# Two blocks on one core: taps moved to TensorE, scaled rows before transposes, head squares in parts

## The chip, the cores and the metric

The kernel runs on one core of one Trainium2 chip. The metric is the device time of one execution in microseconds (us), smaller is better. All tensors that go in and come out are float32.

## The reference, cut to what matters

1,024 tokens of 1,024 channels go through two blocks, one after the other.

```python
def first_block(x):            # names shortened
    h = rmsnorm(x, g); p = h @ w_in                      # 3,072 columns
    d = diff_attention(4 heads, 128 wide); d = rmsnorm(d per head)
    r = silu(gate) * head_rmsnorm(retention(4 heads, 128 wide))
    x = x + concat(d, r) @ w_out
    return x + hier_moe(rmsnorm(x))                      # 32 experts, top 2
def second_block(x):
    h = rmsnorm(rmsnorm(x) of the block before, a_g)     # two norms in a row
    u, v = split(h @ a_w_in + b); g = u * sigmoid(v)     # 8 tiles of 128 channels
    g = depthwise causal convolution of 31 taps over the tokens, per channel
    s = silu(layer_norm(g)); x = x + s @ a_w_out + b
    return x + relu(rmsnorm(x) @ w1) ** 2 @ w2           # 4,096 wide
```

## The kernel before, in words

Nearly every matrix product is a sum of three matmuls on fp32r operands: each float32 operand is split into a rounded upper part (a copy on ACT) and a rest (a subtraction on DVE, for some weights on POOL); `split` and `mm3` (lines 34 to 43) do it. A few products stay plain float32 matmuls on PE.

Phase 1 is the first block up to the router: projections and heads (1a), then `w_out` and the router (1b). Each of the eight heads ends in a norm over its 128 channels, which lie on the partitions. `head_norms` (line 285) squares a head's 128x512 tile on ACT (`osq`), and PE sums the squares over the partitions with a float32 matmul against a matrix of 1/128 (`pm`, line 291, 16 of them in all). Phase 2 runs the 32 experts. Phase 3 (line 1300 on) is the second block.

Phase 3 works on two blocks of 512 tokens, b = 0 and b = 1, and on eight channel tiles, ct = 0 to 7. Its stages, in the order of the driver at the end of the function:

- `first_norms(n)` for n = 0 to 3, 256 tokens each: loads rows `h` (a DMA on POOL), sums squares on ACT (the `junk` activations), makes the reciprocal root on DVE (a chain of twelve small operations, `rs`), and then turns rows into columns on PE (`pt`), from which ACT and DVE write the two parts `xh` and `xl`. Before, the scale of a row enters as a diagonal matrix `dg`: a float32 matmul of the rows against `dg` scales and turns at once. The rows are also scaled in place (`s`) and stored (`x2d`) for the residual.
- `a_in(ct, b)`: two products of 24 matmuls each (`pin`), a sigmoid on ACT (`sig`) and the gated product on DVE (`g`).
- the 31 taps of each channel tile (`conv_steps`). On DVE a tap is one multiply-add over 128x512 (`pc` or `cv`). For ct 4 of b = 0 ACT and POOL do it. For the tiles in `PE_TAPS` a number of the taps of b = 0 run on PE: ACT builds a diagonal of the tap's coefficients, and PE adds a float32 matmul of it with the shifted columns into PSUM.
- `ln(b)`: turns the tiles into rows (`pl`), takes mean and variance on DVE, scales (`cvT`), turns back, silu.
- `a_out(b)`: the product `po`, the residual in `acc`, sums of squares, the reciprocal root, and rows turned to columns with a diagonal per 128 tokens (`pt` again).
- `mlp(b, q)`: products `pf` and `py`; at the last q the results go out by DMA.

Each engine works in order through its own queue. Which instruction stands where in the queues of phase 3 is set by the order in which the code issues and by the scheduler's estimates; two counters of work on PE and DVE (`Counted`) decide how many taps are issued between two products, and `hold()` ties the following instructions of an engine behind the last one. `fill` is a generator that hands out the four products that are kept back from `a_in` of b = 1 for ct 6 and 7; three of its pieces are issued inside `ln(0)` and the last one during `a_out(0)`. Weights (`raw`, three buffers) are split into `whl` on ACT, and then on DVE or, for weights 4 to 15 (`POOL_W`), on POOL.

## Time and profile before

| | us |
|---|---|
| median of 3 runs | 2219.58 |
| lowest, highest | 2219.05, 2225.35 |
| profiled execution, device time | 2219.59 |
| its span | 2217.9 |
| PE busy in the span | 2139.9 (96%) |
| DVE busy | 1631.0 (74%) |
| ACT busy | 1166.6 (53%) |
| POOL busy | 222.2 (10%) |

The span starts with the first instruction and ends with the last; 1.7 us of the device time lie around it. The first 600 us are phases 1a and 1b (they meet at 433 us), the experts end at 1155 us, and phase 3 takes the rest. A matmul on float32 operands leaves two records in the trace, one on fp32r operands one.

### The profile page before, as it was taken

Reading aid. Unit: us, or ns where it says so; the run is one execution under the profiler, and the core shown is the slowest. Engines: PE = TensorE matmul, PEld = TensorE weight load, DVE = VectorE, ACT = ScalarE, POOL = GpSimd, SP = SyncE. Lnnn points to the kernel's source line nnn. Section 1 sums busy time; section 2 is a strip of 40 time slices with the busy share of each in tenths; the row PEclk is TensorE's granted clock in tenths of the full one; section 3 lists DMA queues with packets and bytes.
Section 4 is the critical chain, followed back from the end, with each engine's and each line's share of the span. In section 5 each row is a group of like instructions: output and inputs, shape, how many; then the busy total and the mean of one; then the engine's idle time right before and its main releaser. Section 6 shows DMA issues by size and latency. Waiting matters only on the chain.

```text
span 2217.9 us, 28289 instructions
## 1 busy us (share of the span) xinstructions
PE 2139.9 (96%) x10561; PEld 1743.1 (79%) x10562; DVE 1631.0 (74%) x2538; ACT 1166.6 (53%) x1633; POOL 222.2 (10%) x214
## 2 busy tenths in 40 slices
PE   6999999999699999999988998999999999999998
PEld 5888888788577777777757886988888898888887
DVE  7788755665799999999978998899996634443442
ACT  5565544522588888888866352344333434333431
POOL 0000000010211111121111370000000000000000
PEclk9999999999799999999999999999999999999999
DMA  4111112277799999999974311233332434233331
GB/s 156 41 39 45 49 49 64 80 260 271 284 371 369 359 366 365 358 357 351 367 248 143 101 39 48 77 93 107 105 95 76 126 97 149 86 97 94 108 98 42
DMA packets 194128, 367.62 MB, mean 166 GB/s; under 512 B 15104, under 2 KB 137408, under 8 KB 169408
## 3 DMA queue, kind: packets, MB, share of 16 engines
q1 hardware_dynamic: 177040, 318.01, 41.4%
q0 software_dynamic: 16944, 47.74, 6.7%
q8 instruction: 85, 1.39, 0.3%
q14 instruction: 59, 0.48, 0.1%
HBM read 342.62 MB, written 35.65 MB: 171 GB/s over the span
## 4 chain that ended last, share of the span: by engine, by line
PE 45%; issue 21%; DVE 3%; DMA 3%; ACT 1%; POOL 0%; POOLq 0%; ACTq 0%; DVEq 0%; SPq 0%
PE pin L1265 7%; PE py L1265 6%; PE pf L1265 5%; PE pg L38 5%; PE pg L37 5%; PE pg L36 5%; PE py L36 2%; PE py L38 2%; PE py L37 2%; DMA h<-y,src 2%; PE po L1265 1%; PE pt L1093 1%; DVE cv L1265 1%; PE pt L1265 1%; PE pl L1265 1%
## 5 line engine op out<-in xcount | busy, mean ns | idle before, releaser
L1062 DVE TENSOR_TENSOR wl<-raw,wh 128x1024 fp32r<-128x1024 f32 x384 | 454.4, 1220 | 39.4 <-PE pg L37 24.6
L1061 ACT ACTIVATE wh<-raw 128x1024 fp32r<-128x1024 f32 x384 | 395.9, 1058 | 49.8 <-PE pg L38 27.8
L1265 PE MATMUL py<-whl,hid 128*128 128x512 f32 x1536 | 360.4, 392 | 0.3 <-ACT hid L1265 0.2
L1265 ACT ACTIVATE whl<-raw 128x1024 fp32r<-128x1024 f32 x160 | 168.5, 1057 | 339.4 <-PE py L1265 125.0
L1265 PEld LDWEIGHTS py<-whl,hid 128*128 128x128 f32 x1536 | 285.0, 188 | 65.8 <-ACT hid L1265 5.2
L1265 PE MATMUL pf<-xh,whl 128*128 128x512 f32 x1024 | 318.8, 390 | 0.3 <-DVE whl L1265 0.3
L1265 DVE TENSOR_TENSOR whl<-raw,whl 128x1024 fp32r<-128x1024 f32 x148 | 180.4, 1228 | 144.5 <-ACT whl L1265 143.9
L1265 PEld LDWEIGHTS pf<-xh,whl 128*128 128x128 f32 x1024 | 192.1, 188 | 40.2 <-DVE whl L1265 0.5
L36 PE MATMUL pg<-wh,xth 128*112 128x512 f32 x512 | 204.7, 400 | 0.0
L38 PE MATMUL pg<-wh,xtl 128*112 128x512 f32 x512 | 201.9, 394 | 0.0
L37 PE MATMUL pg<-wl,xth 128*112 128x512 f32 x512 | 201.2, 393 | 0.4 <-DVE wl L1062 0.4
L1265 PE MATMUL pf<-xl,whl 128*128 128x512 f32 x512 | 199.5, 390 | 0.0
L1265 PE MATMUL pin<-xh,whl 128*128 128x512 f32 (+1 forms) x544 | 164.9, 383 | 6.7 <-ACT xh L1265 6.6
L1265 DVE SCALAR_TENSOR_TENSOR cv<-g,cols,cv 128x512 f32<-128x512 f32 x232 | 161.5, 749 | 0.0
L36 PE MATMUL pp<-xhl,wh 128*128 128x512 f32 x384 | 156.6, 408 | 0.0
L37 PE MATMUL pp<-xhl,wh 128*128 128x512 f32 x384 | 151.6, 395 | 0.0
L38 PE MATMUL pp<-xhl,wl 128*128 128x512 f32 x384 | 150.6, 392 | 0.0
L1265 DVE TENSOR_TENSOR acc<-acc,py 128x512 f32<-128x512 f32 x128 | 87.5, 685 | 84.5 <-PE py L1265 84.0
L1265 DVE SCALAR_TENSOR_TENSOR pc<-g,cols,pc 128x512 f32<-128x512 f32 x194 | 135.6, 752 | 3.2 <-ACT pc L1265 1.6
L1265 PEld LDWEIGHTS pin<-xh,whl 128*128 128x128 f32 x544 | 100.8, 190 | 26.1 <-ACT xh L1265 7.8
L1265 ACT ACTIVATE relu<-pf 128x512 f32<-128x512 f32 x64 | 38.0, 594 | 140.0 <-PE pf L1265 137.3
L1265 PEld LDWEIGHTS pf<-xl,whl 128*128 128x128 f32 x512 | 96.2, 188 | 19.8
(435 smaller groups left out, 3859.8 us busy)
## 6 DMA issues: line engine op xcount, KB each, us to landing
raw<-in_expert_w_gate_dram SPq DMA_DIRECT2D x64, 1024.0 KB
raw<-in_expert_w_up_dram SPq DMA_DIRECT2D x64, 1024.0 KB
raw<-in_expert_w_down_dram SPq DMA_DIRECT2D x64, 1024.0 KB
raw<-in_mlp_w_dram SPq DMA_DIRECT2D x128, 512.0 KB
wst<-in_w_in_dram SPq DMA_DIRECT2D x24, 512.0 KB
raw<-in_a_w_in_dram SPq DMA_DIRECT2D x16, 512.0 KB
raw<-in_a_w_out_dram SPq DMA_DIRECT2D x16, 512.0 KB
x<-in_x_dram SPq DMA_DIRECT2D x8, 512.0 KB
```

The costliest lines, as they stand in the source:

```text
L36: nc.tensor.matmul(out, lhsT=ah, rhs=bh, start=first, stop=False)
L37: nc.tensor.matmul(out, lhsT=ah, rhs=bl, start=False, stop=False)
L38: nc.tensor.matmul(out, lhsT=al, rhs=bh, start=False, stop=last)
L1061: s.acts.append(nc.scalar.activation(th, src, AF.Copy))
L1062: lo = nc.vector.tensor_tensor(tl, src, f32(th), op=ALU.subtract)
L1093: last = nc.tensor.transpose(pt[:, j], c.xg[e % XG][:CAP, (4 * q + j) * 128:(4 * q + j + 1) * 128], c.ident[:CAP, :CAP])
L1265: return s.placed(f(*args, **kw))
```

## The change

1. `head_norms`: the matrix of 1/128 is fp32r. Each tile of squares is split into two fp32r parts (`osp`: a copy on ACT, a subtraction on DVE), and two fp32r matmuls take the place of one float32 matmul, 16 times.
2. `PE_TAPS` goes from 10 taps of ct 7 to 8 taps of ct 6 and 20 taps of ct 7, so 28 taps of b = 0 run on PE.
3. `first_norms` and `a_out` no longer build diagonals. Rows are scaled into another tile first, on ACT or DVE (`scaled`), and PE turns them with its transpose operation: 64 transposes in `first_norms`, 64 in the two `a_out`.
4. The driver takes the statistics and the scaling of n = 2 ahead of the second half of `a_in(0, 0)`, and those of n = 3 right behind it.
5. `fill`: two pieces ahead of the layer norm's transposes, one held between their first and second half, and the last one now at the end of `a_out(0)`.
6. The eight last outputs of b = 1 go out from SP's queue and no longer from POOL's.

```diff
-        c.ones_mean = cst2.tile([128, 128], F32, name="ones_mean")
-        V.memset(c.ones_mean, 1.0 / 128)
+        ones = sm.tile([128, 128], F32, tag="state", bufs=2, name="ones")
+        V.memset(ones, 1.0 / 128)
+        c.ones_mean = cst2.tile([128, 128], F32R, name="ones_mean")
+        V.tensor_copy(c.ones_mean, ones)
...
-                nc.tensor.matmul(pm[:, z], lhsT=c.ones_mean, rhs=sq, start=True, stop=True)
+                sp_ = sp.tile([128, 2, 512], F32R, tag="cs0", bufs=4, name="osp")
+                split(nc, sp_[:, 0], sp_[:, 1], sq)
+                for y in range(2):
+                    nc.tensor.matmul(pm[:, z], lhsT=c.ones_mean, rhs=sp_[:, y], start=y == 0, stop=y == 1)
...
-PE_TAPS = {7: 10}
+PE_TAPS = {6: 8, 7: 20}
...
+        def scaled(y, x, r, z):
+            if z:
+                A.activation(y, x, AF.Copy, scale=r)
+            else:
+                V.tensor_scalar(y, x, r, None, op0=ALU.mult)
+            return y
...
-            for j, (y, dg) in enumerate(zip(ys, dgs)):
-                nc.tensor.matmul(pt[:, j * 128:j * 128 + 128], lhsT=y[:, k * 128:(k + 1) * 128], rhs=dg, start=True, stop=True)
+            for j, y in enumerate(ys):
+                nc.tensor.transpose(pt[:, j * 128:j * 128 + 128], y, c.ident)
...
-            dgs = [diagonal(rs[:, 0, 1, z:z + 1]) for z in range(2)]
+            ys = [scaled(h[:, z], s[:, z], rs[:, 0, 1, z:z + 1], z or n) for z in range(2)]
...
-            dgs = [diagonal(rs[:, 0, j:j + 1]) for j in range(4)]
+            ys = []
+            for z in range(2):
+                ys.append([gp[b].tile([128, GW], F32, tag="g", name="y")[:, :512] for _ in mine])
+                for j, i in enumerate(mine):
+                    scaled(ys[z][j], acc[i][:, z * 512:z * 512 + 512], rs[:, 0, j:j + 1], j % 2)
...
-                        nc.gpsimd.dma_start(out=out[0, i * 128:i * 128 + 128, d], in_=acc[i][:, d])
+                        (nc.sync if b else nc.gpsimd).dma_start(out=out[0, i * 128:i * 128 + 128, d], in_=acc[i][:, d])
...
+        next(norm[2])
+        next(norm[2])
         run(a_in(0, 0, 256, 512))
+        next(norm[3])
+        next(norm[3])
         nc.level()
-        next(norm[2])
         run(a_in(1, 0), LEAD, (0,))
         next(norm[2])
-        next(norm[3])
-        next(norm[2])
         run(a_in(2, 0), LEAD, (0,))
-        next(norm[3])
         next(norm[3])
...
         next(fill)
+        next(fill)
         pump(1e9, (0,))
         V.hold()
         for n, _ in enumerate(steps):
-            if n == 0:
-                for _ in range(3):
-                    next(fill)
+            if n == 3:
+                nc.tensor.hold()
+                next(fill)
```

How the queues of phase 3 move is shown at two places. The first is ACT's queue near the start, around the split of the weights for the second product of `a_in(2, 0)`: `whl_13085` in the kernel before. `pin_12946` is the first product of `a_in(1, 0)`, and `pt_13045` to `pt_13072` are the turned rows of n = 2. Before:

```order
L1265 ACTIVATE pc_12971<-g_12769,cols_1181 128x512
L1265 ACTIVATE whl_13085<-raw_12937 128x1024
L1265 ACTIVATE sig_13013<-pin_12946,cols_1181 128x512
L1265 ACTIVATE xh1_12667<-pt_13045,cols_1181 128x256
L1265 ACTIVATE xh1_12667<-pt_13054,cols_1181 128x256
```

In the changed kernel the same weights are `whl_13165`; `pt_13143` and `pt_13152` are the last turned rows of n = 2, and `h_12929` holds the scaled rows of n = 3:

```order
L1270 ACTIVATE sig_13241<-pin_13177,cols_1191 128x512
L1270 ACTIVATE xh1_12733<-pt_13152,cols_1191 128x256
L1270 ACTIVATE h_12929<-s_13014,rs2_13013 128x1024 x2
L1270 ACTIVATE xh1_12733<-pt_13143,cols_1191 128x256
L1270 ACTIVATE xh1_12733<-pt_13152,cols_1191 128x256
L1270 ACTIVATE whl_13165<-raw_13040 128x1024
L1270 ACTIVATE s_13014<-s_13014,rs2_13013 128x1024
```

The split stood ahead of all turned rows of n = 2; now it stands behind all of them and behind the scaling of n = 3.

The second place is PE's queue where these weights are used: `pin_13123` before, `pin_13208` in the changed kernel. Before:

```order
L1265 MATMUL pin_13097<-xh0_12665,whl_12939 128x512
L1265 MATMUL pt_13072<-dg_13032,s_12927 128x128
L1265 MATMUL pt_13072<-dg_13034,s_12927 128x128
L1265 MATMUL pin_13123<-xh0_12665,whl_13085 128x512
L1265 MATMUL pin_13123<-xl0_12666,whl_13085 128x512
```

In the changed kernel:

```order
L1270 MATMUL pin_13177<-xh0_12731,whl_13042 128x512
L1270 MATMUL pt_13152<-ident_65,h_12886 128x128 x2
L1270 MATMUL pt_13143<-ident_65,h_12886 128x128 x2
L1270 MATMUL pt_13152<-ident_65,h_12886 128x128 x2
L1270 MATMUL pt_13246<-ident_65,h_12929 128x128
L1270 MATMUL pin_13208<-xh0_12731,whl_13165 128x512
L1270 MATMUL pin_13208<-xl0_12732,whl_13165 128x512
```

The turned rows are transposes now, the last of them stand together ahead of the product, and a first transpose of n = 3 stands there too. The third matmul of `pin_13208` needs the part of `whl_13165` that POOL writes.

## Rows read from the trace of the kernel before

**Rows 1.** Page, part 1: busy us (share of the span) and instructions of each engine.

```profile
PE 2139.9 (96%) x10561; PEld 1743.1 (79%) x10562; DVE 1631.0 (74%) x2538; ACT 1166.6 (53%) x1633; POOL 222.2 (10%) x214
```

**Rows 2.** Windows of 100 us: length, busy of PE, PEld, DVE, ACT, POOL, PEclk, DMA.

```profile
1100.00:1200.00 100.00, 80.03 (x405) 62.06 (x403) 78.72 (x147) 74.22 (x109) 18.05 (x18) 0.91 0.69 243
1200.00:1300.00 100.00, 99.88 (x472) 83.54 (x471) 93.05 (x144) 44.05 (x70) 45.55 (x30) 1.00 0.24 74
1300.00:1400.00 100.00, 93.26 (x462) 76.22 (x461) 89.48 (x141) 38.81 (x59) 23.77 (x20) 0.97 0.13 43
```

**Rows 3.** Timeline of PE (start, us, instruction): ten taps and their follower; fp32r matmuls.

```profile
1339.91 8.74 PE L1265 MATMUL pc<-g,dg 128*128 128x512 f32 x20
1348.09 0.80 PE L1265 MATMUL pin<-xh,whl 128*128 128x512 f32 x1
1348.73 0.40 PE L1265 MATMUL pin<-xl,whl 128*128 128x512 f32 x1
...
2194.77 17.16 PE L1265 MATMUL py<-whl,hid 128*128 128x512 f32 x75
```

**Rows 4.** Timeline of PE: twelve transposes, and eight matmuls against a diagonal.

```profile
1354.00 1.47 PE L1265 MATMUL pl<-ident,g 128*128 128x128 f32 x12
...
1439.82 1.95 PE L1265 MATMUL pt<-dg,acc 128*128 128x128 f32 x16
```

**Rows 5.** Timeline of PE where phase 1a meets 1b; brackets: idle before, and releaser.

```profile
435.20 1.13 PE L291 MATMUL pm<-osq,ones_mean 128*128 128x512 f32 x2 [1.92 <-ACT osq L290]
436.66 2.07 PE L291 MATMUL pm<-osq,ones_mean 128*128 128x512 f32 x2 [0.34 <-ACT osq L290]
439.98 0.79 PE L36 MATMUL pw<-wo,mh 128*128 128x512 f32 x1 [1.25 <-ACT mh L42]
```

**Rows 6.** Timeline of PE at the start of phase 3.

```profile
1162.86 2.07 PE L1265 MATMUL pt<-dg,s 128*128 128x128 f32 x8 [7.33 <-DVE dg L1265]
...
1197.92 0.40 PE L1265 MATMUL pin<-xl,whl 128*128 128x512 f32 x1
...
1216.57 0.62 PE L1265 MATMUL pin<-xh,whl 128*128 128x512 f32 x2
```

**Rows 7.** Timeline of ACT there: turned rows, squares, scaling, a split of weights.

```profile
1167.93 0.45 ACT L1265 ACTIVATE xh<-pt,cols 128x256 fp32r<-128x256 f32 x1
1168.29 1.04 ACT L1265 ACTIVATE junk<-s 128x1024 bf16<-128x1024 f32 x1
...
1179.09 1.14 ACT L1265 ACTIVATE s<-s,rs 128x1024 f32<-128x1024 f32 x1
...
1195.59 0.46 ACT L1265 ACTIVATE xh<-pt,cols 128x256 fp32r<-128x256 f32 x1
...
1200.42 1.06 ACT L1265 ACTIVATE whl<-raw 128x1024 fp32r<-128x1024 f32 x1 [0.80 <-DMA x2d<-s]
```

**Rows 8.** Timeline of POOL there: its half of two splits.

```profile
1186.21 3.29 POOL L1392 TENSOR_TENSOR whl<-raw,whl 128x1024 fp32r<-128x1024 f32 x1 [3.76 <-ACT whl L1265]
...
1201.56 2.39 POOL L1392 TENSOR_TENSOR whl<-raw,whl 128x1024 fp32r<-128x1024 f32 x1 [3.64 <-ACT whl L1265]
```

**Rows 9.** Windows of 1 us around PE's stop in the layer norm, columns as in rows 2.

```profile
1376.00:1377.00 1.00, 0.00 (x0) 0.00 (x0) 0.93 (x6) 0.77 (x1) 0.00 (x0) 1.00 0.00 0
...
1380.00:1381.00 1.00, 0.88 (x4) 0.69 (x5) 1.00 (x2) 0.00 (x0) 0.00 (x0) 0.50 0.00 0
...
1386.00:1387.00 1.00, 1.00 (x11) 1.00 (x10) 0.69 (x2) 1.00 (x3) 0.00 (x0) 1.00 0.00 0
```

**Rows 10.** Timeline: DVE's last product before the norm; PE behind it and `a_out(0)`.

```profile
1370.73 0.75 DVE L1265 SCALAR_TENSOR_TENSOR g<-pin,cols,sig 128x512 f32<-128x512 f32 x1
...
1380.12 5.49 PE L1265 MATMUL pl<-ident,cvT 128*128 128x128 f32 x24 [5.90 <-DVE cvT L1265]
...
1443.34 2.05 PE L1265 MATMUL pt<-dg,acc 128*128 128x128 f32 x16 [0.96 <-DVE xl L1265]
```

**Rows 11.** Timeline of POOL at the end: the last output.

```profile
2212.95 0.54 POOL L1683 DMA_DIRECT2D out_dram<-acc  x1 [2.18 <-DVE acc L1265]
```

More of the change, by code (lines that the diff above doesn't have):

```diff
@@ L1473, in phase3, with turned @@
         junk = tp[1].tile([128, NB], F32, tag="cv1", name="junk").bitcast(BF16)
-        def diagonal(r):
-            dg = sm.tile([128, 128], F32, tag="dg", name="dg")
-            V.tensor_scalar(dg, c.ident, r, None, op0=ALU.mult)
-            return dg
-        def turned(b, o, k, ys, dgs, gain, pt):
-            for j, (y, dg) in enumerate(zip(ys, dgs)):
-                nc.tensor.matmul(pt[:, j * 128:j * 128 + 128], lhsT=y[:, k * 128:(k + 1) * 128], rhs=dg, start=True, stop=True)
+        def scaled(y, x, r, z):
[4 more added lines that the diff above has]
+            return y
+        def turned(b, o, k, ys, gain, pt):
+            for j, y in enumerate(ys):
+                nc.tensor.transpose(pt[:, j * 128:j * 128 + 128], y, c.ident)
             A.activation(X[b][0][:, k, o], pt, AF.Copy, scale=gain[:, k:k + 1])
@@ L1514, in first_norms @@
                     pt = bank(psl, "pt")
-                turned(b, o, k, [s[:, 0], s[:, 1]], dgs, mixg, pt[:, (k % 2) * 256:(k % 2) * 256 + 256])
+                turned(b, o, k, [y[:, k * 128:k * 128 + 128] for y in ys], mixg, pt[:, (k % 2) * 256:(k % 2) * 256 + 256])
             for z in range(2):
@@ L1642, in a_out @@
             for k in range(8):
-                turned(b, slice(0, NB), k, [acc[i] for i in mine], dgs, mlpg, bank(psl, "pt"))
+                turned(b, slice(0, NB), k, [y[:, k % 4 * 128:k % 4 * 128 + 128] for y in ys[k // 4]], mlpg, bank(psl, "pt"))
             yield 5
```

## Prediction

> **What bounds the kernel now.** I read the page's busy times first, then windows of 100 us, then PE's timeline wherever a window is not full. PE is busy 96% of the span, DVE 74%, ACT 53% [rows 1], and the windows say where the other 4% are: 80.0 us busy of 100 at the start of phase 3, 99.9 while DVE and PE share the convolution, 93.3 around the layer norm [rows 2]. So where PE is full, the time is the sum of PE's work, and what another engine saves there is worth nothing; where PE stops, the time is the chain that it waits for. DVE's 93% beside PE's 99.9% [rows 2] is no second bound: PE never waits for the taps there, and DVE's last gated product ahead of the layer norm starts at 1370.73, before PE's last transposes [rows 10]. There are three stops to look at: where phase 1a meets 1b [rows 5], the start of phase 3 [rows 6], and 5.90 us in the layer norm [rows 10]. Everything behind 1444 us is a PE stream in which the change touches only one set of turned rows.
>
> **The change part by part.** The sum is made against the profiled execution's own 2219.6 us (span 2217.9 and 1.7 around it), which is also the median of the runs.
>
> *Prices.* A 512-column fp32r matmul takes 17.16 / 75 = 0.229 us. Ten float32 taps take 8.18 us to the start of the next record and 8.74 to their own end; the follower's record is 0.80 long against 0.40 for the one behind it, so it began about 0.40 late, and I take (8.18 + 0.40) / 10 = 0.86 each, bounds 0.82 and 0.87 [rows 3]. A transpose takes 1.47 / 12 = 0.123, a turn by a diagonal 1.95 / 8 = 0.244 [rows 4], so each of the 128 replaced saves 0.121 where PE is the bound.
>
> *Taps.* 18 more float32 matmuls on PE: 18 x 0.86 = +15.5 (14.7 to 15.7). On DVE 17 multiply-adds go, but that is off the path, as said above: DVE merely arrives earlier at the layer norm. ACT builds 18 more diagonals, hidden, since ACT is busy 44 us of 100 in that stretch [rows 2].
>
> *Squares.* Two fp32r matmuls for one float32 matmul save 0.86 - 0.458 = 0.40. 14 of the 16 lie in PE's full stretches: -5.6. The extra copies and subtractions lie on ACT and DVE beside them. The last two stand at the boundary of 1a and 1b, where PE stops 1.92, 0.34 and 1.25 us for ACT [rows 5]. The change lets the first products of 1b start between them, but the second square now goes through copy and subtraction first, and the third kind of product needs a part that DVE writes late. If all three stops went, that would be -3.5; a second stop like the first would be +1.9. I take -0.5, near no change, because ACT still does the same squares, split of `m` and splits of `w_out` one behind the other.
>
> *The start of phase 3* is the term that decides. Before, PE's stream of 512-column products runs from 1197.92, and the third matmul of the second product of `a_in(2, 0)` starts at 1216.57 [rows 6]. That matmul needs POOL's half of a split whose ACT half ran at 1200.42 and whose POOL half at 1201.56 [rows 7, 8], 13 us early. In the changed order the ACT half stands behind the turned rows of n = 2 and behind the scaling of n = 3. Count ACT's queue from the first turned rows to the end of that split: 24 `xh` at about 0.45, 10 squares at 1.04, 11 scalings of 1,024 columns at 1.14, 4 splits at 1.06 [rows 7], and what I put at 5 us of sigmoids, a table load and small copies: 10.8 + 10.4 + 12.5 + 4.2 + 5 = 43 us. Before, the first `xh` starts at 1167.93 [rows 7]; now two scalings and a square stand ahead of it and one split fewer, so 1167.9 + 2.3 + 1.0 - 1.0 = 1170.2. The split ends at 1213.2 at the earliest, POOL adds 2.39 [rows 8], hand-overs some 0.4: 1216.0, against 1216.57, so -0.6 at best. At worst ACT waits on the way: for the products behind its sigmoids, and for the root of n = 3, a chain of small DVE operations which now stand one by one between taps. I allow 3.5 us for that, +2.9, and take +1.5. PE itself would be there earlier: by the same prices ACT reaches the last turned rows of n = 1 after some 20 us (16 `xh`, 4 squares, 5 scalings, a split, 2 us of the rest), at 1191 instead of 1195.59 [rows 7]; PE needs 2.3 more, as it did then up to 1197.92, and then the 18.65 us between the two rows of rows 6 less 16 x 0.121: about 1210. So PE stands nearly idle for 6 to 9 us. After the 5.90 us of the layer norm the granted clock is 0.50 (1.2 GHz of 2.4) at 1380 and full again at 1386 [rows 9]: 5.5 us at half speed, 2.7 us lost. I take 2.0, since a few matmuls stand in the gap. The term is +3.5, bounds -0.6 and +6.5. The 48 turned rows ahead of this place are inside it.
>
> POOL's half is 2.39 beside taps and was 3.29 at 1186.21 [rows 8], so the slow row would make the term 0.9 larger. The Trainium skill (SBUF — State Buffer, "Who interferes with whom") says that a VectorE instruction with two SBUF inputs blocks a GpSimd instruction that reads SBUF; the taps there have one input in PSUM, so by it 2.39 holds, and the trace's two rows fit that.
>
> *The other turned rows*: 16 of n = 3 and 64 of the two `a_out`, 80 x 0.121 = -9.7. The added scalings lie on ACT and DVE: in `a_out(0)` behind two products now instead of one (24 x 0.229 = 5.5 more cover), in `a_out(1)` behind products of the MLP.
>
> *The held product* moves 5.5 us of PE work from ahead of the layer norm to behind `a_out(0)`: nothing net. In the norm itself the stop stays: it is DVE's chain of statistics, root and scaling behind PE's last transposes, and one gated product of 0.75 [rows 10] now stands within it: +0.7 (-3 to +1.5, the low end if half the stop went). Behind `a_out(0)` PE stopped 0.96 us for DVE [rows 10]; with shorter turns there is less PE work between DVE's `xl`: +0.5 (-1 to +2).
>
> *The last outputs.* POOL's issue takes 0.54 us [rows 11], all of it at the end; on SP some of it goes: -0.3 (-0.8 to +0.5). The Trainium skill (DMA: Bandwidth & Descriptors, "SWDGE vs HWDGE vs iDMA" and the specifications) gives a first byte after about 1 us from GpSimd's queue and 0.6 from SP's; by it, an estimate, -0.4. No row here shows an output on SP.
>
> Sum: 15.5 - 5.6 - 0.5 + 3.5 - 9.7 + 0.7 + 0.5 - 0.3 = +4.1, so 2223.7. PE's work alone falls by 15.5 - 5.6 - 15.5 = -5.6; it is the late split that turns this round.
>
> **The rivals.** *The stops close (faster).* If ACT does not wait and the split comes in time (-0.6), the boundary's stops all go (-3.5) and half the stop in the norm does (-3): 15.5 - 5.6 - 3.5 - 0.6 - 9.7 - 3 + 0.5 - 0.3 = -6.7, so 2212.9, and less if the norm's stop goes whole: 2210. For it speaks that the driver now takes n = 2 and 3 early and the products of 1b start earlier; against it ACT's 43 us, which are a sum and not a guess.
>
> *The late split at its long end (slower).* If the root of n = 3 comes only when DVE has worked through the taps between its steps, the scaling of n = 3 holds the split, and the term is +6.5 or more; with the boundary's second stop: 4.1 + 3 + 2.4 = +9.5, so 2229. It decides from a stop of about 8 us ahead of `pin_13208`. For it speaks the order of both queues; against it, that before ACT had 56 us of 100 free just behind this place [rows 2].
>
> *The taps are repaid by DVE (the change does what its parts seem made for).* If DVE rather than PE were the bound of the convolution, up to 17 x 0.75 = 12.8 us, by the record of a DVE operation of that shape [rows 10], would come back, and the time would be near 2211. The 99.9 us of PE in 100 [rows 2] speak against it; it shares the chance of the first rival.
>
> **How the numbers follow.** A measurement here tells about 0.3% from no change, 6.7 us: faster is under 2212.9, slower over 2226.2. My forecast, 2223.7, lies within; its own range by the bounds is 2218 to 2228, so a part of it is slower. I give the forecast 0.55, of which 0.13 falls over 2226.2, the slower rival 0.25, the faster cases 0.20. That makes faster 0.18, same 0.45, slower 0.37. Eight in ten reach from 2211 to 2230.
>
> **What would show it.** Right: in the changed profile PE is idle 5 us or more ahead of a `pin` product near 1211 to 1220, released by POOL's `whl`, with a granted clock of 0.50 behind it; `pc` records of 28 taps take some 24 us elapsed; the 16 squares' matmuls take about 0.46 each; the stop in the norm stays near 6 us. Wrong: no stop there, or a layer norm that PE passes without one, or stops at the boundary of 1a and 1b that grow or vanish.

## The result and the profile after

The changed kernel takes 2239.18 us (median of 4 runs, 2238.78 to 2240.34) against 2222.22 for the kernel before in the same comparison: ratio 1.0079, 95% interval 1.0061 to 1.0097, so 14 to 22 us slower. The forecast was 2223.7, with 2211 to 2230 as range: the sign that it leaned to, but the time lies 15 us above the forecast and 9 above the range. The profiled execution of the changed kernel took 2240.3 us (span 2238.7), that of the kernel before 2219.6 (span 2217.9).

Part 1 of the page of the changed kernel answers [rows 1], and the windows of 100 us answer [rows 2] (columns: window, length, busy time of PE, PEld, DVE, ACT, POOL, granted TensorE clock, DMA share, GB/s):

```profile
PE 2148.6 (96%) x10469; PEld 1739.7 (78%) x10470; DVE 1623.9 (73%) x2531; ACT 1193.3 (53%) x1682; POOL 217.6 (10%) x206
```

```profile
1100.00:1200.00 100.00, 79.87 (x386) 60.14 (x385) 76.92 (x117) 75.60 (x109) 14.49 (x17) 0.90 0.74 260
1200.00:1300.00 100.00, 92.55 (x402) 74.08 (x401) 84.56 (x155) 43.74 (x69) 33.69 (x20) 0.95 0.27 84
1300.00:1400.00 100.00, 97.15 (x395) 71.34 (x393) 69.51 (x103) 44.35 (x77) 38.00 (x31) 1.00 0.11 38
```

The window from 1200 us, where PE was busy 99.88 of 100 us, now has 92.55, at a granted clock of 0.95. To see what came earlier, take one landmark, PE's last product of phase 2. From PE's timeline, before and after (start, us, instruction, idle time before it and its releaser):

```profile
1154.40 1.12 PE L1131 MATMUL pa<-y,xg 112*128 112x512 f32 x2 [1.34 <-DVE h L1132]
```

```profile
1160.86 1.12 PE L1136 MATMUL pa<-y,xg 112*128 112x512 f32 x2 [0.74 <-DVE h L1137]
```

So 6.5 us of the 20.8 between the two profiles arose before phase 3, where the prediction had put a gain of 6.1. From the end of that row to the end of the span phase 3 takes 2217.9 - 1155.5 = 1062.4 us before and 2238.7 - 1162.0 = 1076.7 after: 14.3 more, where the prediction's terms make 10.2 (4.1 + 6.1). This length, called phase 3 below, is the best measure of a single profile, as will be seen.

The boundary of phases 1a and 1b, answering [rows 5]:

```profile
440.53 0.80 PE L36 MATMUL pw<-wo,mh 128*128 128x512 f32 x1 [5.96 <-ACT mh L42]
```

PE's start of phase 3, answering [rows 6], and the two engines that it waits for, answering [rows 7, 8]:

```profile
1169.77 0.47 PE L1270 MATMUL pt<-ident,h 128*128 128x128 f32 x1 [7.79 <-DVE h L1270]
1175.26 0.90 PE L1270 MATMUL pt<-ident,h 128*128 128x128 f32 x3 [5.01 <-ACT h L1270]
...
1200.67 0.40 PE L1270 MATMUL pin<-xl,whl 128*128 128x512 f32 x1
...
1219.15 0.44 PE L1270 MATMUL pt<-ident,h 128*128 128x128 f32 x2 [0.96 <-DVE xl L1270]
1221.59 0.33 PE L1270 MATMUL pt<-ident,h 128*128 128x128 f32 x1 [2.00 <-DVE xl L1270]
1222.38 0.79 PE L1270 MATMUL pin<-xh,whl 128*128 128x512 f32 x1 [0.46 <-ACT whl L1270]
...
1224.83 1.22 PE L1270 MATMUL pin<-xh,whl 128*128 128x512 f32 x2 [1.02 <-POOL whl L1397]
...
1234.05 0.50 PE L1270 MATMUL pin<-xh,whl 128*128 128x512 f32 x1 [1.26 <-ACT whl L1270]
...
1236.48 1.22 PE L1270 MATMUL pin<-xh,whl 128*128 128x512 f32 x2 [1.70 <-POOL whl L1397]
```

```profile
1218.47 2.18 ACT L1270 ACTIVATE h<-s,rs 128x1024 f32<-128x1024 f32 x2
1220.55 0.83 ACT L1270 ACTIVATE xh<-pt,cols 128x256 fp32r<-128x256 f32 x2
1221.27 1.06 ACT L1270 ACTIVATE whl<-raw 128x1024 fp32r<-128x1024 f32 x1
...
1232.94 1.06 ACT L1270 ACTIVATE whl<-raw 128x1024 fp32r<-128x1024 f32 x1 [7.58 <-DMA x2d<-s]
```

```profile
1222.41 2.36 POOL L1397 TENSOR_TENSOR whl<-raw,whl 128x1024 fp32r<-128x1024 f32 x1 [8.43 <-ACT whl L1270]
...
1234.08 2.35 POOL L1397 TENSOR_TENSOR whl<-raw,whl 128x1024 fp32r<-128x1024 f32 x1 [7.88 <-ACT whl L1270]
```

The predicted stop is there, at the predicted place: the third matmul of the second product of `a_in(2, 0)` waits for POOL's half until 1224.83. Less the 6.5 us that the whole stage is late, that is 1218.4, where the prediction said 1216.57 + 1.5 = 1218.1. The stop is split up: of the last four waits ahead of this matmul, 4.4 us together, only 1.02 us name POOL (the sign given was 5 us or more, released by POOL's `whl`). The 5.01 us that PE waits for ACT's scaled rows were not foreseen, but they are made up by then: PE's stream of 512-column products starts at 1200.67, which is 1194.2 less the 6.5, ahead of the 1197.92 of the kernel before. What was not foreseen and adds to the time stands behind the predicted stop: a second split is late, because its ACT half waits 7.58 us for a write-out of scaled rows, and PE waits 1.26 and 1.70 us for its two halves. Splits and scaled rows take their buffers from one ring (`pair` in the code). Adding the brackets of all of PE's rows from 1150 to 1260 us gives 27.2 us of stops against 17.7 before, and 24.4 against 16.3 from the end of phase 2 on.

From the end of phase 2 to the layer norm's first transpose the changed kernel takes 220.6 us and the kernel before 198.5. In the two traces the 22.1 us more are 15.0 on the taps, 8.1 of stops and 5.8 on the 720 `pin` matmuls, less 6.7 on the turned rows (each matmul from its start to the next one's start, waits left out). Where the granted clock is 0.50, `pin` matmuls of 512 columns start 0.43 us apart, and 0.23 where it is 1.00. The clock in windows of 5 us there:

```profile
1220.00:1225.00 5.00, 1.93 (x5) 1.03 (x6) 5.00 (x9) 4.52 (x7) 2.59 (x2) 0.73 0.01 2
1225.00:1230.00 5.00, 5.00 (x14) 3.96 (x15) 4.83 (x8) 0.36 (x1) 0.84 (x2) 0.59 0.74 238
1230.00:1235.00 5.00, 3.52 (x16) 2.25 (x14) 2.85 (x6) 1.54 (x3) 0.92 (x1) 1.00 0.20 80
1235.00:1240.00 5.00, 3.52 (x10) 2.82 (x11) 0.66 (x1) 0.00 (x0) 1.43 (x1) 0.66 0.37 105
```

It fell twice to 0.50 (1.2 GHz of 2.4), after either group of stops: in windows of 1 us it is 0.50 from 1223 to 1229 and from 1236 to 1239 us, and windows of 5 us that hold a fall or a rise show values between.

Twenty taps and the layer norm, answering [rows 3, 10]: 20 taps take 17.33 us, and the stop in the norm is 6.06, as predicted.

```profile
1356.08 17.33 PE L1270 MATMUL pc<-g,dg 128*128 128x512 f32 x40
...
1403.20 4.81 PE L1270 MATMUL pl<-ident,cvT 128*128 128x128 f32 x24 [6.06 <-DVE cvT L1270]
```

### The profile page after: what moved, and what is told of

It is laid out like the page before. It is cut to its first block, busy times and chain, and to the rows that moved or that the text cites. A ratio compares the mean times of both kernels' runs of the same rounds, so it can differ in the third digit from the quotient of the medians.

```text
span 2238.7 us, 28136 instructions
## 1 busy us (share of the span) xinstructions
PE 2148.6 (96%) x10469; PEld 1739.7 (78%) x10470; DVE 1623.9 (73%) x2531; ACT 1193.3 (53%) x1682; POOL 217.6 (10%) x206
## 4 chain that ended last, share of the span: by engine, by line
PE 67%; DVE 3%; DMA 2%; ACT 1%; issue 1%; POOL 0%; DVEq 0%; POOLq 0%; ACTq 0%; SPq 0%
PE py L1270 15%; PE pf L1270 13%; PE pin L1270 7%; PE pg L37 5%; PE pg L38 5%; PE pg L36 5%; PE po L1270 4%; PE py L38 3%; PE py L37 3%; PE py L36 3%; PE pt L1098 1%; PE pc L1270 1%; DVE cv L1270 1%; DMA raw<-in_mlp_w_dram 1%; PE pl L1270 1%
## 5 line engine op out<-in xcount | busy, mean ns | idle before, releaser
L1270 DVE SCALAR_TENSOR_TENSOR pc<-g,cols,pc 128x512 f32<-128x512 f32 x177 | 123.1, 750 | 14.7 <-ACT pc L1270 13.4
L37 PEld LDWEIGHTS pg<-wl,xth 128*112 128x112 f32 x512 | 89.8, 175 | 27.6 <-DVE wl L1067 1.3
```

Of the source, the lines that this page charges most:

```text
L37: nc.tensor.matmul(out, lhsT=ah, rhs=bl, start=False, stop=False)
L1270: return s.placed(f(*args, **kw))
```

## The experiments

Kernels `b_...` are the kernel before with an edit, `a_...` the changed kernel with one. Each was timed beside the kernel before on the same chip; ratios are to that, with 95% intervals. An expectation stands ahead of each. The table gives both measures:

```
kernel       median us  ratio to before (interval)   phase 3, us against before's 1062.4
before       2222 to 2224 in each comparison          -
after        2239.2     1.0079 (1.0061 to 1.0097)    +14.3
b_squares    2223.6     1.0005 (0.9993 to 1.0016)    +0.6
b_taps       2235.1     1.0056 (1.0043 to 1.0069)    +17.1
b_first_drv  2229.9     1.0032 (1.0020 to 1.0045)    +6.5
b_first      2238.7     1.0067 (1.0047 to 1.0086)    +16.3
b_aout       2220.1     0.9986 (0.9974 to 0.9997)    -3.7
b_drv        2228.5     1.0029 (1.0017 to 1.0042)    +4.5
b_dve        2222.2     1.0002 (0.9993 to 1.0011)    -1.2
b_first_dve  2227.9     1.0022 (1.0009 to 1.0035)    +7.2
b_sq_dve     2228.9     1.0032 (1.0020 to 1.0044)    +0.4
a_taps       2228.2     1.0026 (1.0017 to 1.0036)    +4.6
a_dve        2230.2     1.0033 (1.0018 to 1.0047)    +5.5
a_squares    2236.6     1.0057 (1.0040 to 1.0074)    +13.5
a_x2d        2240.7     1.0082 (1.0069 to 1.0094)    +15.4
best         2224.6     1.0007 (0.9994 to 1.0020)    +0.7
best2        2215.8     0.9964 (0.9949 to 0.9979)    -6.8
best3        2217.3     0.9976 (0.9967 to 0.9985)    -5.1
best4        2220.0     0.9992 (0.9981 to 1.0004)    -0.6
```

**The squares alone.**

```diff
-                nc.tensor.matmul(pm[:, z], lhsT=c.ones_mean, rhs=sq, start=True, stop=True)
+                sp_ = sp.tile([128, 2, 512], F32R, tag="cs0", bufs=4, name="osp")
+                split(nc, sp_[:, 0], sp_[:, 1], sq)
+                for y in range(2):
+                    nc.tensor.matmul(pm[:, z], lhsT=c.ones_mean, rhs=sp_[:, y], start=y == 0, stop=y == 1)
...
```

> The kernel before with the head squares in parts alone. In the changed kernel's trace everything up to the last product of phase 2 is 6.5 us later than before (1160.86 against 1154.40), although the matmuls of the squares take less time. Theory A, the squares themselves do that (a longer chain behind each square, PE waiting for it around 435 us and then for the router's transposes, with stretches at half clock): 5 to 7 us slower than before, and the profile shows a granted clock well under 1.00 between 35 and 45 us and again near 510 and 545 us. Theory B, the clock that fell at 35 us and the stops of phase 1b are chance, which differs from run to run and not from kernel to kernel: the time is 3 to 5 us below before (16 matmuls at 0.86 become 32 that add up to some 3.9 us less), with the clock at 1.00 between 35 and 45 us. Theory C, both: within 2 us of before.

Theory C: 1.0005, no difference (0.9993 to 1.0016). The time from the first square's matmul to the end of phase 1a is 322.8 us, in the changed kernel 322.7, and 324.1 in the kernels with whole squares: 1.3 us of gain instead of 5.6. Two reasons can be read. PE's timeline of the kernel before, and of b_squares:

```profile
303.93 1.88 PE L291 MATMUL pm<-osq,ones_mean 128*128 128x512 f32 x4
305.24 0.79 PE L36 MATMUL pp<-xhl,wh 128*128 128x512 f32 x1
```

```profile
123.45 0.39 PE L296 MATMUL pm<-osp,ones_mean 128*128 128x512 f32 x1
...
228.82 0.38 PE L36 MATMUL po<-ah,vh 128*128 128x256 f32 x1 [0.22 <-ACT ah L42]
...
441.59 0.79 PE L36 MATMUL pw<-wo,mh 128*128 128x512 f32 x1 [6.62 <-ACT mh L42]
442.18 0.63 PE L37 MATMUL pw<-wo,mh 128*128 128x512 f32 x1
```

Two whole squares take 1.31 to the next start and leave it 0.40 late: 0.855 each, as priced. The 28 matmuls of the split ones stand singly or in small groups among other products, and from each to the next start passes 0.23 to 0.43 us; together 8.0, so 0.29 each and not 0.229. That leaves 14 x 0.855 - 8.0 = 4.0 us on PE. And PE waits 2.9 us in all up to the end of phase 1a instead of 1.5, for ACT's parts `ah` three times (1.3 us). The rest of the way from 2.6 to 1.3 I can't place. At the boundary the three stops of [rows 5], 3.5 us together, become one of 6.62 for ACT and one of 0.53 for `osp`; in both kernels the first products behind them start 0.43 us apart. The tenth product of phase 1b starts 334.5 us behind the first square's matmul in both. So by then nothing is left.

**Does ACT's added copy take it back?** Here the squares are split as in b_squares, but DVE squares, and ACT only copies.

```diff
-                A.activation(sq, o, AF.Square)
+                V.tensor_tensor(sq, o, o, op=ALU.mult)
```

> The kernel before with the head squares in parts, as in b_squares, but the squaring itself on DVE, so that ACT only makes the copy and has no more to do than before. Theory A, ACT's added copies are what took back the squares' gain: the 1.3 us of waits for ACT in phase 1a and most of the 6.6 us stop for ACT at the boundary go, the end of phase 1a comes at most 321.5 us behind the first square's matmul (324.1 under the kernel before, 322.8 with the squares on ACT), and the time is 2 to 6 us below before. Theory B, the way of a square through copy and subtraction is the cost, on whatever engine: the stops stay, now for DVE, and the time is within 2 us of before or slower.

Slower by 4 to 10 us, and the waits for `ah` stay (1.42 us); PE now also waits for the squares' own parts, 3.2 us up to the end of phase 1b. Theory A falls by the time. Its landmark can't be used: the end of phase 1a comes 318.6 us behind the first square's matmul, but that matmul itself starts at 120.0 us instead of 112.2. What is shown is only that the longer way of a square is no better on DVE.

**The start of phase 3: order and scaled rows together, then apart.** First both, as in the change:

```diff
-            dgs = [diagonal(rs[:, 0, 1, z:z + 1]) for z in range(2)]
+            ys = [scaled(h[:, z], s[:, z], rs[:, 0, 1, z:z + 1], z or n) for z in range(2)]
...
+        next(norm[2])
+        next(norm[2])
         run(a_in(0, 0, 256, 512))
+        next(norm[3])
+        next(norm[3])
         nc.level()
...
```

> The kernel before with the first norms' rows scaled ahead of transposes and with the changed order of norms and products at the start of phase 3; no other part. Theory A, the start of phase 3 costs what the two traces give (20.8 us at the end, less 6.5 ahead of phase 3, 15.4 of taps, and plus 7.7 for the turned rows of the two output parts: +6.6): 5 to 8 us slower than before, with PE stopped twice for POOL's part of a split, near 1217 and 1229 us, and a granted clock near 0.5 behind each. Theory B, these stops came in the changed kernel because phase 2 ended late there and would not be here: no stop for POOL, and the time some 2 to 8 us below before, since 64 turned rows become 0.121 us shorter each.

Theory A: both stops for POOL are there (1.01 and 1.71 us), 4 to 10 us slower, phase 3 +6.5. The clock, with PE's busy time, in this kernel:

```profile
1200.00:1220.00 20.00, 15.52 (x67) 11.52 (x66) 18.59 (x44) 15.24 (x25) 4.52 (x5) 0.87 0.26 86
1220.00:1240.00 20.00, 17.19 (x71) 12.88 (x70) 11.22 (x20) 4.75 (x9) 4.74 (x2) 0.87 0.33 109
```

Under the kernel before both windows have a clock of 1.00 and PE is full. So the stage pays twice: 7.8 us more of stops, and up to 5 us by the clock (0.13 of these 40 us; the 720 `pin` matmuls ahead of the norm take 4.2 us longer in all). Against that stand 64 shorter turned rows, 6.7 us. Scaled rows alone, in the old order:

```diff
-            dgs = [diagonal(rs[:, 0, 1, z:z + 1]) for z in range(2)]
+            ys = [scaled(h[:, z], s[:, z], rs[:, 0, 1, z:z + 1], z or n) for z in range(2)]
```

> The kernel before with the first norms' rows scaled ahead of transposes, in the old order of norms and products; no other part. Theory A, the order is what makes the splits late: no stop for POOL's part of a split between 1200 and 1240 us, the stream of 512-column products begins within 3 us of before's 1197.92, and the time lies between 5 us below before and 1 us above (32 turned rows in a full stretch save 3.9, the scaling ahead of the first transposes costs up to 2). Theory B, the scalings on ACT (1.14 us each, where a diagonal took a short DVE operation) are what makes the splits late: PE stops for POOL here too, and it is 4 to 8 us slower than before.

Both expectations were too low: 10 to 19 us slower. PE waits 13.7 us for ACT's scaled rows, nearly all of it in three places, and 1.21 for POOL:

```profile
1172.98 0.90 PE L1265 MATMUL pt<-ident,h 128*128 128x128 f32 x3 [4.24 <-ACT h L1265]
...
1210.79 0.44 PE L1265 MATMUL pt<-ident,h 128*128 128x128 f32 x2 [2.30 <-ACT h L1265]
...
1238.81 0.69 PE L1265 MATMUL pt<-ident,h 128*128 128x128 f32 x2 [6.48 <-ACT h L1265]
```

The changed order alone, with diagonals:

```diff
+        next(norm[2])
+        next(norm[2])
         run(a_in(0, 0, 256, 512))
+        next(norm[3])
+        next(norm[3])
         nc.level()
...
```

> The kernel before with nothing but the changed order of norms and products at the start of phase 3; its turned rows still go by diagonals. With the scaled rows this order gave 25.5 us of PE stops between 1150 and 1260 us (17.7 under the kernel before), and the scaled rows in the old order gave 31.6. Theory A, the order makes the splits of the weights late: PE stops for POOL's part of a split here too, 21 to 26 us of stops, 2 to 7 us slower than before. Theory B, the order is sound and the scalings on ACT are what is slow: no stop for POOL, 14 to 18 us of stops, within 2 us of before or faster.

Theory B in the stops, with none for POOL and 16.3 us in all at the start (17.7 before); theory A in the time, 4 to 9 us slower. So the stops at the start don't explain the loss. Of phase 3's 4.5 us, 1.45 are a stop for DVE's statistics at the layer norm, and 2.2 lie on the same products and turned rows at the start, which take longer without a longer stop; why wasn't traced further. The stop at the norm:

```profile
1359.89 0.66 PE L1265 MATMUL pl<-ident,g 128*128 128x128 f32 x4 [1.45 <-DVE bst L1265]
```

Then the scalings on DVE, in the changed order:

```diff
-            ys = [scaled(h[:, z], s[:, z], rs[:, 0, 1, z:z + 1], z or n) for z in range(2)]
+            ys = [scaled(h[:, z], s[:, z], rs[:, 0, 1, z:z + 1], 0) for z in range(2)]
```

> The kernel before with the first norms' rows scaled ahead of transposes and the changed order, as in b_first_drv, but all scalings on DVE, none on ACT. Theory A, the load that the scalings put on ACT is what costs (6.3 us of PE waiting for ACT's scaled rows, and the splits that ACT reaches late): the stops between 1150 and 1260 us fall from 25.5 to under 20, and the time is 3 to 7 us below that of b_first_drv. Theory B, the order and the longer way to the first transpose cost as much on either engine: 24 to 28 us of stops, the time within 2 us of b_first_drv.

Theory A in the time (2222.2, 7.7 below b_first_drv) and in the cause: no stop for POOL, 20.3 us of stops (under 20 were expected). DVE's timeline: it scales two rows in 1.42 us, where ACT took 2.18 in the changed kernel (its row at 1218.47 above):

```profile
1184.47 1.42 DVE L1265 TENSOR_SCALAR h<-s,rs 128x1024 f32<-128x1024 f32 x2
```

The same edit in the changed kernel:

> The changed kernel with the first norms' scalings all on DVE, none on ACT; no other edit. Theory A, ACT's scalings are what makes the start of phase 3 slow in the changed kernel (there PE stops 27.2 us between 1150 and 1260 us, among it 6.3 for ACT's scaled rows and 4.4 for the two late splits): no stop for POOL, at most 21 us of stops, and 5 to 9 us below the changed kernel's 2239.2, as much as the same edit gave on the kernel before (2229.9 to 2222.2). Theory B, in the changed kernel something else holds the start (what ends late in phase 2, or DVE, which now carries the scalings): within 2 us of 2239.

2230.2, 9 us below the changed kernel's 2239.2, and no stop for POOL; 21.7 us of stops, a little over what was expected. So of the 17 us that the change costs, half is the choice of engine for these scalings. Last, DVE's scalings in the old order:

> The kernel before with the first norms' rows scaled ahead of transposes, all scalings on DVE, in the old order of norms and products. The order cost 6 us by itself (2228.5 against 2222.3), and on the changed order the scalings on DVE gave 2222.2. Theory A, the order and the scaled rows add up: 3 to 8 us faster than before, without a stop for POOL. Theory B, in the old order the scaled rows come too late whichever engine scales them (with ACT this order was 14.9 us slower than before): 2 to 10 us slower.

Theory B: 2 to 8 us slower, with 11.6 us of waits for DVE's scaled rows and a stop of 1.70 for POOL. Order and scaled rows don't add up. In phase 3's length: diagonals 0 in the old order and +4.5 in the new; scaled on ACT +16.3 and +6.5; scaled on DVE +7.2 and -1.2. The new order is worth 8 to 10 us where rows are scaled, and costs 4.5 where they aren't.

**The write-outs.** The second split waits for a buffer whose rows POOL writes out behind its own half of the split before. Here ACT issues them:

```diff
-                nc.gpsimd.dma_start(out=x2d[i * 128:i * 128 + 128, :], in_=s[:, z])
+                A.dma_start(out=x2d[i * 128:i * 128 + 128, :], in_=s[:, z])
```

> The changed kernel with the write-outs of the first norms' scaled rows issued by ACT instead of POOL; ACT's order shifts a little with it. Theory A, the second late split waits for a buffer whose rows POOL writes out late: ACT's half of that split comes 2 us earlier or more against the split before it (11.7 us apart in the changed kernel), the second stop for POOL shrinks by as much or goes, and the time is 2 to 5 us below the changed kernel's 2239.2. Theory B, ACT's own queue sets it, and the issues (about 0.55 us each) only lengthen it: within 1 us of 2239 or above.

Theory B in the time: 2240.7. The halves of the two splits on ACT come 10.2 us apart instead of 11.7, but the second still waits for the landing, and PE for it:

```profile
1230.59 1.06 ACT L1270 ACTIVATE whl<-raw 128x1024 fp32r<-128x1024 f32 x1 [4.86 <-DMA x2d<-s]
```

```profile
1234.13 0.73 PE L1270 MATMUL pin<-xh,whl 128*128 128x512 f32 x1 [1.70 <-POOL whl L1397]
```

The scheduler moved other work of ACT with the issues, and PE waits 5.2 us for DVE's `xl` instead of 3.2. The buffer is one link of that chain; that it is the whole of it isn't shown.

**The taps**, alone and taken out of the changed kernel:

```diff
-PE_TAPS = {7: 10}
+PE_TAPS = {6: 8, 7: 20}
```

> The kernel before with 28 taps on TensorE instead of 10, no other part. Theory A, PE bounds the convolution and DVE's saved multiply-adds are worth nothing: 15.4 us slower than before (18 at 0.855), the stop ahead of the layer norm between 5 and 6.5 us. Theory B, DVE bounds part of the stretch or the norm behind it and its 17 saved operations come back in part: 3 to 10 us slower, with a shorter stop in the layer norm.

9.6 to 15.3 us slower. The profile has theory A's numbers (8 taps and 20 take 24.0 us with the lateness of their followers, 0.86 each; the stop in the norm is 5.91), but its execution is the longest of the six runs (2231.7 to 2239.3).

> The changed kernel with 10 taps on TensorE as before, instead of 28. Alone, the 18 more taps cost 9.6 to 15.3 us by the runs. Theory A, they cost their PE time whatever stands around them (18 times 0.855): 14 to 16 us below the changed kernel's 2239.2, so about 2224. Theory B, in the changed kernel's order DVE needs the relief: 5 to 11 us below, about 2231.

11 us below the changed kernel, theory B's end. DVE is late ahead of the norm here, and PE stops a second time:

```profile
1381.72 1.76 PE L1270 MATMUL pl<-ident,g 128*128 128x128 f32 x7 [4.54 <-DVE g L1270]
1389.06 3.20 PE L1270 MATMUL pl<-ident,cvT 128*128 128x128 f32 x13 [5.58 <-DVE cvT L1270]
```

The changed order of the start alone doesn't do that. b_first_drv has it too, with 10 taps, and PE stops only once in the norm:

```profile
1378.18 1.58 PE L1265 MATMUL pl<-ident,g 128*128 128x128 f32 x13
1386.14 5.54 PE L1265 MATMUL pl<-ident,cvT 128*128 128x128 f32 x24 [6.38 <-DVE cvT L1265]
```

There three products (72 `pin` matmuls) stand between the first and last of these transposes, in a_taps two (48): the third is held back by `fill` until behind `a_out(0)`, and the piece that stays between the halves is only a gated product on DVE. So it seems to be with that product moved that DVE needs the relief, and then the taps buy back some 4 of their 15.4 us (10.1 us of stops in the norm against 6.06). The move by itself was not tried.

**The squares taken out of the changed kernel.**

> The changed kernel with the head squares whole, as before; no other edit. Theory A, the squares in parts gain nothing (alone they gave 2223.6 against 2223.6): within 3 us of the changed kernel's 2239.2, and the time from the first square's matmul to the last product of phase 1a is again 324.1 us instead of 322.7. Theory B, by the prediction's sum they save 6.1 us: about 2245. Theory C, they are what costs the 6.5 us ahead of phase 3 in the changed kernel's profile: about 2233.

2236.6, 2.6 below the changed kernel, where runs of both overlap. Theory B is excluded. By the interval alone (2231 to 2239 us) theory C isn't, but b_squares excludes it.

**The turned rows of the output parts.**

```diff
-            dgs = [diagonal(rs[:, 0, j:j + 1]) for j in range(4)]
+                for j, i in enumerate(mine):
+                    scaled(ys[z][j], acc[i][:, z * 512:z * 512 + 512], rs[:, 0, j:j + 1], j % 2)
...
-                turned(b, slice(0, NB), k, [acc[i] for i in mine], dgs, mlpg, bank(psl, "pt"))
+                flipped(b, slice(0, NB), k, [y[:, k % 4 * 128:k % 4 * 128 + 128] for y in ys[k // 4]], mlpg, bank(psl, "pt"))
```

> The kernel before with the rows of the two output parts scaled ahead of transposes; no other part. Theory A, PE is full there and the 64 shorter turns count whole: 64 times 0.121 is 7.7 us less, 5 to 8 us faster than before. Theory B, the 8 scalings of each part lengthen the way from the statistics to the first transpose on ACT and DVE, and PE stops there (under the kernel before it stops 0.96 us behind the first part): 3 us faster to 2 us slower, with a stop of some us ahead of the first transposes.

0.7 to 5.8 us faster, phase 3 -3.7: between the theories. Four turns by a diagonal take 0.80 us to the next start (kernel before), four transposes 0.36 (b_aout):

```profile
1836.61 1.05 PE L1265 MATMUL pt<-dg,acc 128*128 128x128 f32 x8
1837.41 0.94 PE L1265 MATMUL py<-whl,hid 128*128 128x512 f32 x3
```

```profile
1652.74 7.57 PE L1265 MATMUL py<-whl,hid 128*128 128x512 f32 x32 [1.06 <-ACT hid L1265]
...
1842.23 0.60 PE L1265 MATMUL pt<-ident,y 128*128 128x128 f32 x4
1842.59 1.17 PE L1265 MATMUL py<-whl,hid 128*128 128x512 f32 x4
```

That is 0.11 a row, 7.0 for 64. But behind the first part's turned rows PE now stops 3.4 us in all up to the end, 0.8 before, and 2.1 of it are for ACT's `hid` in the MLP. Why ACT is late there wasn't tried.

**Versions meant to beat both.** `best` is b_first_dve with b_aout; `best2` is b_dve with b_aout and the last outputs on SP; `best3` is best2 with one of the first two scalings on ACT; `best4` is best2 with ACT issuing the write-outs.

> The kernel b_first_dve with the rows of the two output parts scaled ahead of transposes too (alone 3.1 us faster than before): meant as the version that beats both. Theory A, the gains add up: 6 to 11 us faster than before, 2211 to 2216. Theory B, the start of phase 3 takes back what the turned rows give: within 3 us of before or slower.

Theory B, for the reason shown at b_first_dve.

> The kernel before with the scaled rows of the first norms and of the output parts, the changed order of norms and products, all first scalings on DVE, and the outputs of the second block on SP; 10 taps and whole squares as before. Theory A, the parts add up (0 for the start of phase 3 in this form, 3.1 us for the output parts): 2 to 5 us faster than before, about 2219. Theory B, the gain of the output parts is lost in stops behind it: within 1.5 us of before.

Faster than the kernel before by 4.7 to 11.3 us, more than expected, and 23 below the changed kernel. Its phase 3 is the sum of its parts: -1.2 for the start, -3.7 for the output parts, and -1.9 for the outputs on SP. The last is read at the end, from DVE's last addition to the end of the span: 5.26 us under the kernel before and 3.33 under best2, and the same in every profile here, 11 with the outputs on POOL's queue and 8 on SP's. The rows of the one and the other (spans 2217.9 and 2215.1):

```profile
2211.97 0.69 DVE L1265 TENSOR_TENSOR acc<-acc,py 128x512 f32<-128x512 f32 x1 [2.03 <-PE py L1265]
```

```profile
2211.11 0.69 DVE L1265 TENSOR_TENSOR acc<-acc,py 128x512 f32<-128x512 f32 x1 [2.03 <-PE py L1265]
```

> As best2, but the second of the two scalings of the first 256 rows runs on ACT, beside DVE's; the other six stay on DVE. Theory A, the first transposes of phase 3 wait for DVE's two scalings one after the other (12.8 us of waiting for DVE's scaled rows in b_dve), and sharing the first pair saves 1 to 1.5 us: 1 us below best2. Theory B, ACT has its squares to do at that time and the second row comes no earlier: within 1 us of best2 or later.

2217.3, within 1.5 us of best2: no gain by sharing. PE then waits 4.8 us for ACT's row and 9.0 for DVE's, 13.8 together, where it waits 12.8 for DVE's in best2.

> best2 with the write-outs of the first norms' scaled rows issued by ACT instead of POOL. best2 has no stop for a late split. Theory A, the write-outs are off the path there: within 2 us of best2's 2215.8. Theory B, ACT is the engine that PE waits for at the start of phase 3 (5.3 us in best2 for its turned rows), and the issues lengthen that: 2 to 4 us slower than best2.

2220.0, 4.2 us above best2: theory B in the time, but not in its cause. The wait for ACT's turned rows is 5.4 us as before; what comes back are the stops for late splits, 2.7 us for POOL's halves and 2.6 for ACT's.

## Why the prediction was wrong

Set beside each other, by the ratios and an execution of 2222 us: squares and boundary -6.1 predicted, +1.1 measured (-1.6 to +3.6); start of phase 3 with its 64 turned rows +1.6 (3.5 - 16 x 0.121), measured +7.1 (4.4 to 10.0); taps +15.5, measured +12.4 (9.6 to 15.3); turned rows of the output parts -7.2 (64 x 0.121, less 0.5 behind `a_out(0)`), measured -3.1 (-5.8 to -0.7). These four measured make +17.5, the outputs on SP take 1.9 off, and the whole change is +17.6 (13.6 to 21.6). Each of the four is known to about 2.7 us and their sum to about 5, so that the parts account for the whole is shown no more closely than that. By phase 3's length the start, the taps, the turned rows and the outputs make 6.5 + 17.1 - 3.7 - 1.9 = 18.0, and the whole +14.3. The held product was not tried apart.

*The squares: a mis-sized term, the largest.* "Two fp32r matmuls for one float32 matmul save 0.86 - 0.458 = 0.40" took the price of an fp32r matmul from a long run of equal ones [rows 3]; these stand singly or in small groups and cost 0.29. And "The extra copies and subtractions lie on ACT and DVE beside them" was wrong: PE waits 1.4 us more up to the end of phase 1a, and 7.1 instead of 3.5 at the boundary. So the -5.6 came as -1.3, and the boundary's -0.5 as +1.3 up to the tenth product of phase 1b; its bound, a second stop, came in another form, as one long one for ACT. Which of the added operations holds PE up stays open, since with the squaring on DVE the waits for `ah` stayed.

*The start of phase 3: right in mechanism and place, mis-sized.* The late split stood within 0.3 us of where ACT's count and the 1.5 taken for its waits put it; that it came so near is in part luck, since in b_first_drv, with the same order, the place is 0.5 us late and not 1.8. But +3.5 was one split and one gap. Behind that place stands a second late split with 3.0 us of stops: ACT's queue was counted, the ring of buffers that splits share with scaled rows was not. The clock was put at 2.0 for one gap; it fell twice, and the `pin` matmuls took 5.8 us longer. The slower rival had this mechanism and 2229, which would have been the better forecast; its price was still too low, since it too thought of one stop.

*The taps: right in price on PE* (0.86 each). "DVE merely arrives earlier" held for the kernel before; with one product fewer ahead of the norm DVE is late, and the rival "repaid by DVE" is right to some 4 us. So "The held product moves 5.5 us of PE work [...]: nothing net" holds with 28 taps and, by a_taps, not with 10.

*The turned rows: right in price* (0.11 against 0.121 a row), wrong in that all of it would count: 2.6 us came back as stops behind the first part.

*The layer norm* came as predicted, 6.06 for 5.90. *The last outputs* were put at -0.3 and gave -1.9. The estimate from the Trainium skill (DMA: Bandwidth & Descriptors, "Specifications"), 0.4 by its first-byte latencies, agrees in sign, but the measured difference is nearly five times that, so the measurement decides.

*The base.* 2219.6 is at the low end of what the kernel before takes: its later medians are 2222 to 2224, single runs 2217 to 2232. That alone is 3 us of the miss.

And one reading of the two profiles would have misled: the 6.5 us ahead of phase 3 look like the squares' doing. They aren't. From the first square's matmul to the end of phase 2 the 13 profiles with whole squares take 1041.2 to 1051.6 us, 1047.2 in the mean, and the five with squares in parts on ACT 1044.9 to 1050.2, 1047.7 in the mean; b_squares, whose code up to phase 3 is that of the changed kernel, has the shortest of the five.

## What to carry to other kernels

Price an instruction by rows where it stands as it will stand, singly or in a run, and before a chain on another engine is called hidden, look whose result PE waits for next. Where a part lengthens a chain (scaling ahead of transposes), count the buffers that the chain holds as well as its engine's queue, and try the engine that does the work in less time first: with the scalings on DVE the same change costs nothing at the start of phase 3. Parts that are losses or gains by themselves need not add up: the new order pays only with scaled rows, and the scaled rows come out even only in the new order and on DVE.

## What was not expected of the hardware

The clock after one and the same stop differs from run to run. PE stops about 3.4 us for ACT near 36 us in these kernels, with the same instructions around it; two windows of 5 us, in b_first_drv and in b_first (whose code is the same up to phase 3):

```profile
35.00:40.00 5.00, 1.55 (x14) 1.32 (x13) 4.66 (x7) 3.53 (x7) 0.00 (x0) 1.00 0.00 0
40.00:45.00 5.00, 5.00 (x32) 4.23 (x30) 4.62 (x14) 3.92 (x11) 0.00 (x0) 1.00 0.00 0
```

```profile
35.00:40.00 5.00, 1.56 (x10) 1.32 (x9) 4.47 (x7) 3.43 (x6) 0.00 (x0) 0.80 0.00 0
40.00:45.00 5.00, 5.00 (x25) 4.96 (x24) 3.56 (x7) 3.26 (x7) 0.00 (x0) 0.52 0.00 0
```

With the fall the first square's matmul starts at 111.9 us, without it at 109.2: 2.7 us that no code decides. Of the 19 profiles six have no fall there. The Trainium skill (TensorE: Matmul & The Clock Gate, "Part 1: The HAM clock gate") says that the gate's timing isn't tied to the kernel's start, so that the point where it switches shifts from run to run; these rows agree, though no run here shows the cause. Phase 1b adds some us of its own, through stops for ACT's `xt` that come once in the kernel before and four times in best3, whose code is the same up to there. A term of 3 us in this kernel is told by a stage's own length or by many runs, not by where a landmark stands in two profiles.
